# Strassen's seven products for half of the down projection of a two-layer trunk, on one core

## The chip, the cores and the metric

The kernel runs on 1 core of one Trainium2 chip (trn2). The metric is device time in microseconds (us) of one execution; the time of a version is the median over its runs. Besides, one execution is profiled, and its trace gives the start and duration of every instruction. PE is TensorE (PEld its weight loads), DVE is VectorE, ACT is ScalarE, POOL is GpSimd, SP is SyncE, which issues nearly all DMAs.

## The reference

Two layers of a trunk on 256 tokens of width 1024, in float32. Each layer has token mixers (pooling, short convolution, differential attention), a squared-ReLU MLP and an input embedding. The change lies in the MLP:

```python
m = rms_norm(h, norm_mlp_g[i])
h = h + jnp.square(jax.nn.relu(m @ w_up[i])) @ w_down[i]
```

`w_up` is 1024 x 4096 and `w_down` 4096 x 1024 in each of the two layers.

## The kernel before, in words

**Split numbers.** Every operand of a big matmul is a sum of two float32r parts, hi and lo: hi is the rounded value, lo the rest. A product is three matmuls: hi x hi, hi x lo, lo x hi.

**The weight stream.** All big weights come in the order of `weight_plan` (L49), in units of 128 x 1024 numbers; one DMA on SP's queue brings two units (1 MB) into a `stage` tile, of which there are three. `WeightStream.prefetch` (L134) splits a unit: ACT casts it to `whi` (L145), then DVE subtracts to get `wlo` (L146). There are five buffers for each of `whi` and `wlo`; `take` (L153) asks for a unit's successors up to four ahead (`AHEAD = 4`). So the cast of a unit waits until PE has done with the unit whose buffer it takes, and the split of a unit waits for its cast.

**The MLP stage** of a layer (L815 to L875) takes the 4096 hidden features in eight blocks of 512.
- Up units: `first_up` (block 0, four units of 24 matmuls of 256 columns, L285 to L289) and, for blocks 1 to 7, `unit_c` (L292): one unit gives 128 features for all 256 tokens, with 8 matmuls of 512 columns (L298) and 8 of 256 (L300), into one PSUM bank of the pool `bp`, which has four banks. `relu_sq_c` (L828) empties the bank and makes the squared ReLU: an ACT copy (L834), a DVE addition (L835), a DVE multiplication (L836), then `split` (L341: ACT L342, DVE L343).
- Down units: `add_down(j, f)` (L844) multiplies block j, for both token halves, with half f of the 1024 output columns: two units of `unit_a` (L266), each of 12 matmuls of 512 columns (L272 to L274). All blocks add up in four PSUM banks of the pool `acc`, one for each token half t and column half f. `mlp_residual` (L850) scales the sums by 1/mean square and adds them to h (L852).

The order is: the up units of block j, then the down units of block j - 1 for both f. The framework's scheduler sets the final order on each engine; each engine then goes through its list in order.

Of the kernel before, what the change touches and what calls it, by code (L numbers as in the profile page):

```python
# [14 lines left out]
P = 128  # L15
S = 256
# [15 lines left out]
UNIT_COLS = {"A": 512, "B": 256, "C": 128, "P": 512}  # L32
# [16 lines left out]
def weight_plan():  # L49

# [7 lines left out]
    for i in range(DEPTH):  # L58
        def a(name, ks, c):
            plan.extend(("A", name, i, k, c) for k in ks)  # L60
# [27 lines left out]
        for j in range(1, 9):  # L88
            if j < 8:
                plan.extend(("C", "w_up", i, 0, c) for c in range(j * 512, (j + 1) * 512, P))  # L90
            for f in range(2):
                a("w_down", (4 * j - 4, 4 * j - 2), f * 512)
# [5 lines left out]

class WeightStream:

# [5 lines left out]
    def __init__(self, ctx, tc, w):  # L106
        self.nc = tc.nc
        self.w = w
        self.plan = weight_plan()
        self.stage_pool = ctx.enter_context(tc.tile_pool(name="wstage", bufs=self.STAGE_BUFS))  # L110
        self.part_pool = ctx.enter_context(tc.tile_pool(name="wpart", bufs=self.AHEAD + 1))
        self.keep_pool = ctx.enter_context(tc.tile_pool(name="wkeep", bufs=1))
        self.stage = {}
        self.parts = {}
        self.next_dma = 0
        self.next_split = 0
        self.pos = 0

    def load(self, parts=1, between=None):


        if self.next_dma < len(self.plan):
            t = self.stage_pool.tile([P, 2 * UNIT], F32, tag="stage", name="stage")
            src = self.w[self.next_dma // 2]
            n = 2 * UNIT // parts
            for c in range(0, 2 * UNIT, n):
# [3 lines left out]
            for u in range(2):  # L130
                self.stage[self.next_dma + u] = t[:, u * UNIT:(u + 1) * UNIT]
            self.next_dma += 2

    def prefetch(self, upto, between=None):  # L134
        while self.next_split < min(len(self.plan), upto):
# [14 lines left out]
            if u % 2 == 1:  # L150
                self.load()
# [11 lines left out]
def kernel(  # L163
# [42 lines left out]
    def t2(dt=F32):  # L206
        return u2.tile([P, 512], dt, tag="t2", name="t2")

# [57 lines left out]
    def unit_a(accs, xh, xl, name, i, k, c, kx, first, last):  # L266

        wh, wl = ws.take("A", name, i, k, c)
        order = [(t, j) for j in range(2) for t in range(NT)] if first else [(t, j) for t in range(NT) for j in range(2)]
        for t, j in order:  # L270
            tk = slice(t * P, (t + 1) * P)
            nc.tensor.matmul(accs[t], lhsT=xh[:, kx + j, tk], rhs=wh[:, j, :], start=first and j == 0, stop=False)  # L272
            nc.tensor.matmul(accs[t], lhsT=xh[:, kx + j, tk], rhs=wl[:, j, :], start=False, stop=False)  # L273
            nc.tensor.matmul(accs[t], lhsT=xl[:, kx + j, tk], rhs=wh[:, j, :], start=False, stop=last and j == 1)  # L274
# [85 lines left out]
    for i in range(DEPTH):  # L360
# [437 lines left out]
        def mlp_stats():  # L798
            st["r2"] = small(2, "r2")
            nc.vector.reciprocal(out=st["r2"], in_=mean_eps(st["ss"]))  # L800

# [13 lines left out]

        def relu_sq(m):
# [6 lines left out]
            s2 = t2().rearrange("p (m t) -> p m t", t=S)  # L823
# [4 lines left out]
        def relu_sq_c(j, m):  # L828
# [4 lines left out]
            z, s2 = t2()[:, 0:S], t2()[:, 0:S]  # L833
# [9 lines left out]

        def add_down(j, f):  # L844
            for k in (0, 2):
                u = add(lambda k=k: unit_a(get(("d", f)), *st["s", j], "w_down", i, 4 * j + k, f * 512, k,
                                           j == 0 and k == 0, j == 7 and k == 2))
            return u
# [17 lines left out]
        for j in range(1, 9):  # L866
            if j < 8:
# [3 lines left out]
            for f in range(2):  # L871
                u = add_down(j - 1, f)
                if j == 8:
                    at(u, mlp_residual, f)
                    at(u + 1, ple_norm, f)  # L875
                    at(u + 3, lambda f=f: stats_half(st["ss"], f))
# [70 lines left out]
def _pack(inp):  # L947
    import numpy as np

    units = []  # L950
    for kind, name, i, k, c in weight_plan():
        if kind == "P":
            units.append(np.concatenate([inp["pool_w"][i].transpose(1, 0, 2).reshape(P, 4 * P),
                                         inp["p"][i, 0].T.reshape(2, P, S).transpose(1, 0, 2).reshape(P, 2 * S)],
                                        axis=1))
            continue
        wt = inp[name][i]
        nc_ = UNIT_COLS[kind]
        nk = UNIT // nc_
        blk = wt[k * P:(k + nk) * P, c:c + nc_].reshape(nk, P, nc_).transpose(1, 0, 2)  # L960
        units.append(blk.reshape(P, UNIT))
    w = np.stack(units).reshape(-1, 2, P, UNIT).transpose(0, 2, 1, 3).reshape(-1, P, 2 * UNIT)
# [40 lines left out]
```

## Time and profile before

| | us |
|---|---|
| median of 3 runs (lowest to highest) | 859.71 (859.28 to 859.99) |
| the profiled execution, its own time | 859.99 |
| span of its trace (first to last instruction) | 858.2 |
| PE busy in the span | 851.2 (99%) |
| DVE, ACT busy | 582.4 (68%), 454.8 (53%) |
| granted TensorE clock, mean | 1.000 |

A matmul's record is longer than its share of PE, since matmuls overlap: what one costs is the distance from its start to the next one's. The same holds of DVE and ACT, whose instructions start a little before the one ahead of them ends.

### The profile page before, as it was taken

The page shows a single profiled execution, that of the slowest core. Times are in us where ns is not written, and L with a number is a line of the kernel's source. Part 1 is how long each engine was busy: PE and PEld are TensorE (multiplying, and loading weights), DVE is VectorE, ACT ScalarE, POOL GpSimd, SP SyncE. Part 2 cuts the span into 40 slices and gives each one's busy share as a digit, 9 for nine tenths or more (in the row PEclk, how much of TensorE's full clock was granted, in tenths as well). Part 3 has the DMA queues.
Part 4 walks back from the last instruction along what each step waited for, and adds up shares of the span by engine and source line. Part 5 has one row for each costly group of instructions (what it writes and reads, how often), then busy time and mean ns, then how long its engine had stood idle before and what let it go on. Part 6 is the DMA issues. An engine that isn't in the chain of part 4 may idle for free.

```text
span 858.2 us, 11637 instructions
## 1 busy us (share of the span) xinstructions
PE 851.2 (99%) x4564; PEld 733.9 (86%) x4564; DVE 582.4 (68%) x894; ACT 454.8 (53%) x691; POOL 30.6 (4%) x34
## 2 busy tenths in 40 slices
PE   8999999999999999999999999999999999999998
PEld 6989988888888888888889998888889888888887
DVE  5887886656676666666678877955666666666664
ACT  6664564454654444445664746544546544444462
POOL 2400000000000000000023000000000000000000
PEclk9999999999999999999999999999999999999999
DMA  8754536554555555555455444455554555555531
GB/s 319 288 197 157 186 103 216 185 207 174 192 170 185 193 193 196 196 196 189 157 195 196 162 182 147 148 199 192 197 187 157 196 196 197 192 179 186 184 142 50
DMA packets 24103, 158.45 MB, mean 185 GB/s; under 512 B 2800, under 2 KB 3568, under 8 KB 5488
## 3 DMA queue, kind: packets, MB, share of 16 engines
q1 hardware_dynamic: 23904, 157.66, 51.8%
q8 instruction: 36, 0.59, 0.3%
q14 instruction: 19, 0.16, 0.1%
q10 hardware_dynamic: 144, 0.05, 0.0%
HBM read 156.64 MB, written 1.05 MB: 184 GB/s over the span
## 4 chain that ended last, share of the span: by engine, by line
PE 98%; DMA 1%; SPq 0%; DVE 0%; ACT 0%; issue 0%
PE acc L273 20%; PE acc L274 20%; PE acc L272 20%; PE bp L298 12%; PE bp L300 6%; PE bp L289 4%; PE bp L287 4%; PE bp L285 4%; PE tr L321 1%; PE acc L919 1%; DMA stage<-in_w_dram 1%; PE acc L606 1%; PE tr L452 1%; PE tr L698 0%; PE acc L540 0%; PE acc L539 0%
## 5 line engine op out<-in xcount | busy, mean ns | idle before, releaser
L146 DVE TENSOR_TENSOR wlo<-stage,whi 128x1024 fp32r<-128x1024 f32 (+1 forms) x296 | 359.1, 1215 | 239.3 <-ACT whi L145 238.1
L145 ACT CAST whi<-stage 128x1024 fp32r<-128x1024 f32 (+1 forms) x296 | 308.2, 1045 | 348.1 <-PE acc L274 185.3
L272 PE MATMUL acc<-whi,t 128*128 128x512 f32 x752 | 294.1, 393 | 1.4 <-ACT t L311 0.8
L273 PE MATMUL acc<-wlo,t 128*128 128x512 f32 x752 | 293.8, 391 | 0.5 <-DVE wlo L146 0.5
L274 PE MATMUL acc<-whi,t 128*128 128x512 f32 x752 | 290.3, 391 | 0.0
L272 PEld LDWEIGHTS acc<-whi,t 128*128 128x128 f32 x752 | 140.9, 188 | 30.6 <-ACT whi L145 1.8
L273 PEld LDWEIGHTS acc<-wlo,t 128*128 128x128 f32 x752 | 141.3, 188 | 30.0 <-DVE wlo L146 1.8
L274 PEld LDWEIGHTS acc<-whi,t 128*128 128x128 f32 x752 | 140.9, 188 | 29.0
L298 PE MATMUL bp<-t,whi 128*128 128x512 f32 x448 | 122.0, 394 | 0.0
L285 PE MATMUL bp<-t,whi 128*128 128x256 f32 x320 | 90.5, 284 | 0.0
L287 PE MATMUL bp<-t,whi 128*128 128x256 f32 x320 | 90.5, 283 | 0.0
L289 PE MATMUL bp<-t,wlo 128*128 128x256 f32 x320 | 90.5, 283 | 0.0
L298 PEld LDWEIGHTS bp<-t,whi 128*128 128x128 f32 x448 | 77.4, 189 | 11.0
L300 PEld LDWEIGHTS bp<-t,wlo 128*128 128x128 f32 x448 | 68.6, 189 | 9.3
L300 PE MATMUL bp<-t,wlo 128*128 128x256 f32 x448 | 71.2, 281 | 0.0
L287 PEld LDWEIGHTS bp<-t,whi 128*128 128x128 f32 x320 | 61.1, 191 | 0.5
L285 PEld LDWEIGHTS bp<-t,whi 128*128 128x128 f32 x320 | 61.0, 191 | 0.5
L289 PEld LDWEIGHTS bp<-t,wlo 128*128 128x128 f32 x320 | 61.1, 191 | 0.1
L311 ACT ACTIVATE t<-tr,par 128x256 fp32r<-128x256 f32 (+1 forms) x56 | 26.1, 501 | 21.0 <-PE tr L452 8.4
L312 DVE SCALAR_TENSOR_TENSOR t<-tr,par,t 128x256 fp32r<-128x256 f32 (+1 forms) x56 | 27.7, 515 | 5.4 <-ACT t L311 5.1
L343 DVE TENSOR_TENSOR t<-t,t 128x256 fp32r<-128x256 f32 (+1 forms) x64 | 28.6, 449 | 0.0
L342 ACT CAST t<-t 128x256 fp32r<-128x256 f32 (+1 forms) x64 | 27.4, 432 | 0.0
(130 smaller groups left out, 525.1 us busy)
## 6 DMA issues: line engine op xcount, KB each, us to landing
stage<-in_w_dram SPq DMA_DIRECT2D x145, 1024.0 KB, 4.8
stage<-in_w_dram SPq DMA_DIRECT2D x4, 256.0 KB, 5.2
stage<-in_w_dram SPq DMA_DIRECT2D x2, 512.0 KB, 9.3
h<-in_x_dram SPq DMA_DIRECT2D x4, 256.0 KB, 10.6
t<-in_xT_dram SPq DMA_DIRECT2D x1, 512.0 KB, 10.4
out_dram<-h SPq DMA_DIRECT2D x2, 256.0 KB, 2.0
out_dram<-h SPq DMA_DIRECT2D x4, 128.0 KB, 1.8
t<-in_xT_dram SPq DMA_DIRECT2D x1, 384.0 KB, 5.6
```

Source lines behind the costliest of these rows:

```text
L145: self.nc.scalar.copy(out=hi[:, cs], in_=src[:, cs])
L146: self.nc.vector.tensor_sub(out=lo[:, cs], in0=src[:, cs], in1=hi[:, cs].bitcast(F32))
L272: nc.tensor.matmul(accs[t], lhsT=xh[:, kx + j, tk], rhs=wh[:, j, :], start=first and j == 0, stop=False)
L273: nc.tensor.matmul(accs[t], lhsT=xh[:, kx + j, tk], rhs=wl[:, j, :], start=False, stop=False)
L274: nc.tensor.matmul(accs[t], lhsT=xl[:, kx + j, tk], rhs=wh[:, j, :], start=False, stop=last and j == 1)
L285: nc.tensor.matmul(bp[:, m, :], lhsT=wh[:, j, ms], rhs=xh[:, kx + j, :], start=first, stop=False, skip_group_check=True)
L287: nc.tensor.matmul(bp[:, m, :], lhsT=wh[:, j, ms], rhs=xl[:, kx + j, :], start=False, stop=False, skip_group_check=True)
L289: nc.tensor.matmul(bp[:, m, :], lhsT=wl[:, j, ms], rhs=xh[:, kx + j, :], start=False, stop=last, skip_group_check=True)
L298: nc.tensor.matmul(bank, lhsT=wh[:, k, :], rhs=xk[k], start=k == 0, stop=False, skip_group_check=True)
L300: nc.tensor.matmul(bank[:, 1, :], lhsT=wl[:, k, :], rhs=xk[k][:, 0, :], start=False, stop=k == KD - 1, skip_group_check=True)
L312: nc.vector.scalar_tensor_tensor(out=lo, in0=src, scalar=g, in1=hi.bitcast(F32), op0=ALU.mult, op1=ALU.subtract)
L343: nc.vector.tensor_sub(out=lo, in0=src, in1=hi.bitcast(F32))
```

## The change

Blocks are taken in pairs (0,1), (2,3), (4,5), (6,7). For the pairs (0,1) and (4,5) of each layer the down projection is a 2 x 2 matrix product: activations by token half (t) and block, weights by block and column half (f). Instead of eight quarter products of 12 matmuls each it takes Strassen's seven (in Winograd's form), of 12 matmuls each. Product n is two units of a new kind "S", with 6 matmuls a unit.
- **Weight sums.** Products 1, 3 and 2 use a quarter of `w_down` as it is. Products 5, 6, 4 and 7 use sums of quarters, made in two tiles of their own (`fst`, `snd`, 128 x 2048, of the pool t8): quarters (0,0) and (0,1) are loaded into them; after product 1's split DVE adds `snd` to `fst` (product 5); then three DMAs with addition, on POOL's queue, add a further quarter: to `snd` after that addition (product 7), to `fst` after product 5's split (product 6) and again after product 6's (product 4).
- **Activation sums.** `operands` makes four combinations of the squared ReLUs of both blocks, each one DVE instruction of 512 columns and a `split` (one of ACT, one of DVE). The squared ReLUs are kept for it.
- **Where products go.** 2, 3 and 4 add into the `acc` banks of (0,0), (0,1) and (1,0). Products 1, 6 and 7 add up in one `bp` bank ("chain") which DVE reads after each of them; 5 has a `bp` bank ("five") that ACT copies out. From these, `product_out` adds to h what the `acc` banks don't hold.
- **Order.** The eight up units of blocks j and j + 1 come first, then steps of two up units (of blocks j + 2, j + 3) or one half of a down block, with one or two products behind each.
- Units that stay (`add_down` of blocks 2, 3, 6, 7; all up units) have the matmuls that they had.

The core of the diff:

```diff
+GROUPS = (0, 4)
+def mlp_order():
+    order = []
+    for j in range(0, 8, 4):
+        order += [("up", b, m) for b in (j, j + 1) for m in range(4)]
+        ups = [[("up", b, m), ("up", b, m + 1)] for b in (j + 2, j + 3) for m in (0, 2)]
+        downs = [[("down", b, f)] for b in (j + 2, j + 3) for f in range(2)]
+        prods = [[("S", j, n) for n in ns] for ns in ((1,), (5,), (3,), (6,), (7, 2), (4,))]
+        for n, step in enumerate(ups + downs):
+            order += step
+            order += prods[n] if n < len(prods) else []
+    return order
...
     def load(self, parts=1, between=None):
-        if self.next_dma < len(self.plan):
-            t = self.stage_pool.tile([P, 2 * UNIT], F32, tag="stage", name="stage")
...
+            if kind == "S" and prod == 1:
+                if i not in self.sums:
+                    self.sums[i] = self.new_sums()
+                t, second = self.sums[i]
+            elif block:
+                t = self.stage_pool.tile([P, 2 * UNIT], F32, tag="stage", name="stage")
+            else:
+                t = self.sums[i][prod == 7]
...
+            if kind == "S" and prod == 1:
+                self.nc.sync.dma_start(out=second, in_=self.w[self.place[quarter(i, j, 0, 1)]])
...
+    def add_to(self, t, i, j, h, f):
+        self.nc.gpsimd.dma_start(out=t, in_=self.w[self.place[quarter(i, j, h, f)]], accum_op=ALU.add)
+    def sums_after(self, u):
+        kind, prod, i, k, j = self.plan[u]
+        if kind != "S" or k != 2:
+            return
+        fst, snd = self.sums[i]
+        if prod == 1:
+            self.nc.vector.tensor_add(out=fst, in0=fst, in1=snd)
+            self.add_to(snd, i, j, 1, 1)
+        elif prod == 5:
+            self.add_to(fst, i, j, 1, 1)
+        elif prod == 6:
+            self.add_to(fst, i, j, 1, 0)
...
+    ws.new_sums = lambda: [t8().rearrange("p k t -> p (k t)") for _ in range(2)]
...
+    def unit_s(bank, xh, xl, prod, i, k, j, started):
+        wh, wl = ws.take("S", prod, i, k, j)
+        for n in range(2):
+            first = k + n == 0 and not started
+            nc.tensor.matmul(bank, lhsT=xh[:, k + n, :], rhs=wh[:, n, :], start=first, stop=False, ...)
+            nc.tensor.matmul(bank, lhsT=xh[:, k + n, :], rhs=wl[:, n, :], start=False, stop=False, ...)
+            nc.tensor.matmul(bank, lhsT=xl[:, k + n, :], rhs=wh[:, n, :], start=False, stop=k + n == 3, ...)
...
+        def operands(j, step):
+            t0, t1 = slice(0, P), slice(P, S)
+            even, odd = st["f", j], st["f", j + 1]
+            d = t2().rearrange("p (k t) -> p k t", t=P)
+            if step == 0:
+                nc.vector.tensor_sub(out=d, in0=odd[:, :, t1], in1=even[:, :, t1])
...
+            parts = [t2(F32R).rearrange("p (k t) -> p k t", t=P) for _ in range(2)]
+            split(*parts, d)
+            ops[(5, 6, 3, 7)[step]] = parts
...
+        def product_out(n):
+            if n == 5:
+                ops["five"] = t2()
+                nc.scalar.copy(out=ops["five"], in_=tiles.pop(("bp", "five"))...)
+                return
+            chain = tiles[("bp", "chain")].rearrange("p m t -> p (m t)")
+            if n == 1:
+                residual_part(0, 0, chain, "r2")
+                return
+            v = ops["five"] if n == 7 else t2()
+            nc.vector.tensor_add(out=v, in0=chain, in1=ops["five"])
+            if n == 7:
+                residual_part(1, 0, chain, "r2")
...
+            residual_part(n == 7, 1, v, "nr2")
...
-        for j in range(1, 9):
-            if j < 8:
-                for m in range(4):
-                    u = add(lambda j=j, m=m: unit_c(get(("bp", "up", j, m)), st["x"], "w_up", i, j * 512 + P * m))
-                    at(u, relu_sq_c, j, m)
-            for f in range(2):
-                u = add_down(j - 1, f)
...
+        for what, j, n in mlp_order():
+            if what == "up" and j:
+                u = add(lambda j=j, m=n: unit_c(get(("bp", "up", j, m)), st["x"], "w_up", i, j * 512 + P * m))
+                at(u, relu_sq_c, j, n)
+                if j - 1 in GROUPS and n == 3:
+                    for step in range(4):
+                        at(u + 1 + step, operands, j - 1, step)
+            elif what == "down":
+                u = add_down(j, n)
...
+            elif what == "S":
+                add_product(j, n)
```

In the lists below a name's number tells one buffer or bank from another. L244 of the change is the split that was L146; L963, L964 and L459 are L835, L836 and L343 of before; L414 and L416 are L298 and L300.

**DVE, layer 0, up units of blocks 2 and 3.** Before, with two splits and then the empty-and-square work of one up unit in turn:

```order
L146 TENSOR_TENSOR wlo_2510<-stage_2411,whi_2509 128x1024
L146 TENSOR_TENSOR wlo_2540<-stage_2411,whi_2539 128x1024
L835 TENSOR_TENSOR t2_2531<-bp_2508,t2_2531 128x256
L836 SCALAR_TENSOR_TENSOR t2_2532<-t2_2531 128x256
L146 TENSOR_TENSOR wlo_2570<-stage_2458,whi_2569 128x1024
L835 TENSOR_TENSOR t2_2561<-bp_2538,t2_2561 128x256
L343 TENSOR_TENSOR t4_2530<-t2_2532,t4_2529 128x256
L836 SCALAR_TENSOR_TENSOR t2_2562<-t2_2561 128x256
```

And the end of the same place in the change, from the second split of product 5 to the instruction that empties the bank bp_2474 of an up unit:

```order
L244 TENSOR_TENSOR wlo_2528<-t8_2211,whi_2527 128x1024
L1028 SCALAR_TENSOR_TENSOR h00_85<-bp_2510,r2_2309,h00_85 128x512
L244 TENSOR_TENSOR wlo_2547<-stage_2356,whi_2546 128x1024
L459 TENSOR_TENSOR t2_2462<-t2_2459,t2_2461 128x512
L963 TENSOR_TENSOR t2_2467<-bp_2438,t2_2467 128x256
L244 TENSOR_TENSOR wlo_2575<-stage_2356,whi_2574 128x1024
L964 SCALAR_TENSOR_TENSOR t2_2468<-t2_2467 128x256
L996 SCALAR_TENSOR_TENSOR t2_2497<-t2_2459,t4_2275 128x512
L459 TENSOR_TENSOR t4_2466<-t2_2468,t4_2465 128x256
L459 TENSOR_TENSOR t2_2500<-t2_2497,t2_2499 128x512
L244 TENSOR_TENSOR wlo_2605<-stage_2414,whi_2604 128x1024
L963 TENSOR_TENSOR t2_2503<-bp_2474,t2_2503 128x256
```

Splits of shorter units, operand sums (L996, L459 at 512 columns) and an addition to h (L1028) now stand between the instructions that empty the banks.

**PE, the same place in the change**: the last matmul groups of the up unit in bank bp_2573, then product 5 (bank bp_2603).

```order
L414 MATMUL bp_2573<-t8_2154,whi_2475 128x512 x4
L416 MATMUL bp_2573<-t8_2154,wlo_2476 128x256 x4
L385 MATMUL bp_2603<-whi_2511,t2_2461 128x512
L387 MATMUL bp_2603<-wlo_2512,t2_2461 128x512
L389 MATMUL bp_2603<-whi_2511,t2_2462 128x512
```

Product 3 (bank acc_2688) follows 5 at once, before the next up units, and then the first matmul of product 6:

```order
L389 MATMUL acc_2688<-whi_2614,t2_2524 128x512
L385 MATMUL bp_2510<-whi_2690,t2_2499 128x512
L414 MATMUL bp_2628<-t8_2093,whi_2546 128x512 x4
L416 MATMUL bp_2628<-t8_2093,wlo_2547 128x256 x4
L414 MATMUL bp_2628<-t8_2154,whi_2546 128x512 x4
```

With "chain" and "five" held, two of the four `bp` banks are left to the up units there.

## Rows read from the trace of the kernel before

**Rows 1.** The page: busy time of each engine; the chain that ended last
```profile
PE 851.2 (99%) x4564; PEld 733.9 (86%) x4564; DVE 582.4 (68%) x894; ACT 454.8 (53%) x691; POOL 30.6 (4%) x34
...
PE 98%; DMA 1%; SPq 0%; DVE 0%; ACT 0%; issue 0%
PE acc L273 20%; PE acc L274 20%; PE acc L272 20%; PE bp L298 12%; PE bp L300 6%; PE bp L289 4%; PE bp L287 4%; PE bp L285 4%; PE tr L321 1%; PE acc L919 1%; DMA stage<-in_w_dram 1%; PE acc L606 1%; PE tr L452 1%; PE tr L698 0%; PE acc L540 0%; PE acc L539 0%
```

**Rows 2.** Windows, 260.48 to 282.60: busy us (instructions) of PE, PEld, DVE, ACT, POOL, clock, DMA
```profile
260.48:282.60 22.12, 22.12 (x113) 18.82 (x112) 13.90 (x20) 10.70 (x16) 0.00 (x0) 1.00 0.54 191
```

**Rows 3.** All waits of PE in the span: total us, times, longest
```profile
PE tr L224 <- POOL ones L220: 1.0, 1, 1.0
PE acc L272 <- ACT t L311: 0.8, 1, 0.8
PE acc L272 <- ACT whi L145: 0.6, 2, 0.3
PE acc L273 <- DVE wlo L146: 0.5, 1, 0.5
```

**Rows 4.** Waits of DVE and of ACT between 235 and 400
```profile
DVE wlo L146 <- ACT whi L145: 58.1, 58, 1.5
ACT whi L145 <- PE bp L298: 25.3, 20, 1.5
```

**Rows 5.** Timeline of PE: start, us, instruction
```profile
255.72 0.39 PE L272 MATMUL acc<-whi,t 128*128 128x512 f32 x1
...
260.26 0.39 PE L274 MATMUL acc<-whi,t 128*128 128x512 f32 x1
260.48 1.07 PE L298 MATMUL bp<-t,whi 128*128 128x512 f32 x4
...
271.68 0.40 PE L272 MATMUL acc<-whi,t 128*128 128x512 f32 x1
```

**Rows 6.** Timeline of DVE, back to back
```profile
239.94 0.68 DVE L822 TENSOR_SCALAR t<-bp 128x512 f32<-128x512 f32 x1
240.54 0.68 DVE L826 TENSOR_TENSOR t<-t,t 128x512 fp32r<-128x512 f32 x1
241.14 2.35 DVE L146 TENSOR_TENSOR wlo<-stage,whi 128x1024 fp32r<-128x1024 f32 x2
...
248.76 0.42 DVE L343 TENSOR_TENSOR t<-t,t 128x256 fp32r<-128x256 f32 x1
249.09 0.42 DVE L835 TENSOR_TENSOR t<-bp,t 128x256 f32<-128x256 f32 x1
...
398.44 1.40 DVE L852 SCALAR_TENSOR_TENSOR h<-acc,r,h 128x512 f32<-128x512 f32 x2
```

**Rows 7.** Timeline of ACT, back to back
```profile
237.71 1.05 ACT L145 CAST whi<-stage 128x1024 fp32r<-128x1024 f32 x1 [3.96 <-PE bp L287]
238.67 0.63 ACT L824 ACTIVATE t<-t 128x512 fp32r<-128x512 f32 x1
239.20 0.62 ACT L825 ACTIVATE t<-t 128x512 f32<-128x512 f32 x1
...
247.79 0.37 ACT L834 COPY t<-bp 128x256 f32<-128x256 f32 x1
248.06 0.41 ACT L342 CAST t<-t 128x256 fp32r<-128x256 f32 x1
```

**Rows 8.** DMA queue and DMA issues: KB each, median us to landing
```profile
q1 hardware_dynamic: 23904, 157.66, 51.8%
...
stage<-in_w_dram SPq DMA_DIRECT2D x145, 1024.0 KB, 4.8
...
h<-in_x_dram SPq DMA_DIRECT2D x4, 256.0 KB, 10.6
```

**Rows 9.** Groups by line and form: busy us, mean ns of one
```profile
L146 DVE TENSOR_TENSOR wlo<-stage,whi 128x1024 fp32r<-128x1024 f32 x292 | 356.4, 1222 | 237.5 <-ACT whi L145 236.3
...
L835 DVE TENSOR_TENSOR t<-bp,t 128x256 f32<-128x256 f32 x56 | 23.4, 417 | 0.0
```

More of the change, by code (lines that the diff above doesn't have):

```diff
@@ L96, in weight_plan, with quarter, transfer_plan, weight_blocks @@
     return plan
+def quarter(i, j, h, f):
+    return tuple(("A", "w_down", i, 4 * (j + h) + k, 512 * f) for k in (0, 2))
+def transfer_plan():
+    out = []
+    plan = weight_plan()
+    u = 0
+    while u < len(plan):
+        if plan[u][0] != "S":
+            n = 2 if u + 1 < len(plan) and plan[u + 1][0] != "S" else 1
+            out.append((tuple(range(u, u + n)), tuple(plan[u:u + n])))
+        else:
+            n = 2
+            _, prod, i, _, j = plan[u]
+            at = {1: (0, 0), 3: (1, 1), 2: (1, 0)}.get(prod)
+            out.append(((u, u + 1), at and quarter(i, j, *at)))
+        u += n
+    return out
+def weight_blocks():
+    place = {}
+    for _, block in transfer_plan():
+        if block:
+            place.setdefault(block, len(place))
+    for i in range(DEPTH):
+        for j in GROUPS:
+            place.setdefault(quarter(i, j, 0, 1), len(place))
+    return place
 class WeightStream:
@@ L109, in __init__ @@
         self.plan = weight_plan()
+        self.transfers = transfer_plan()
+        self.place = weight_blocks()
+        self.last_unit = {units[-1]: n for n, (units, _) in enumerate(self.transfers)}
         self.stage_pool = ctx.enter_context(tc.tile_pool(name="wstage", bufs=self.STAGE_BUFS))
@@ L119, in load @@
     def load(self, parts=1, between=None):
-        if self.next_dma < len(self.plan):
-            t = self.stage_pool.tile([P, 2 * UNIT], F32, tag="stage", name="stage")
-            src = self.w[self.next_dma // 2]
-            n = 2 * UNIT // parts
-            for c in range(0, 2 * UNIT, n):
+        while self.next_dma < len(self.transfers):
+            units, block = self.transfers[self.next_dma]
+            self.next_dma += 1
+            kind, prod, i, _, j = self.plan[units[0]]
+            size = len(units) * UNIT
+            if kind == "S" and prod == 1:
[4 more added lines that the diff above has]
+                t = self.stage_pool.tile([P, 2 * UNIT], F32, tag="stage", name="stage")
+            else:
+                t = self.sums[i][prod == 7]
+            for n, u in enumerate(units):
+                self.stage[u] = t[:, n * UNIT:(n + 1) * UNIT]
+            if not block:
+                continue
+            src = self.w[self.place[block]]
+            n = size // parts
+            for c in range(0, size, n):
                 self.nc.sync.dma_start(out=t[:, c:c + n], in_=src[:, c:c + n])
@@ new lines, in product @@
+        def product(j, n, k):
+            half = {1: (0, 0), 2: (0, 1), 4: (1, 1)}.get(n)
+            if half:
+                parts = [v[:, :, half[0] * P:(half[0] + 1) * P] for v in st["s", j + half[1]]]
+            else:
+                parts = ops[n]
+            into = {2: (0, 0), 3: (0, 1), 4: (1, 0)}.get(n)
+            if into:
+                t, f = into
+                unit_s(get(("d", f))[t], *parts, n, i, k, j, k > 0 or not begin(t, f))
+            elif n == 5:
+                unit_s(get(("bp", "five"))[:].rearrange("p m t -> p (m t)"), *parts, n, i, k, j, False)
+            else:
+                unit_s(get(("bp", "chain"))[:].rearrange("p m t -> p (m t)"), *parts, n, i, k, j, n > 1)
@@ L848, in add_down, with add_product @@
+        def add_product(j, n):
+            for k in (0, 2):
+                u = add(product, j, n, k)
+            if n in (1, 5, 6, 7):
+                at(u, product_out, n)
             return u
```

109 lines of the change are left out of this document (78 added, 31 removed).

## The prediction, made before the changed kernel ran

> **What bounds the kernel now.** I read the page first, then the waits, then single stretches. The page shows PE busy 99% of the span and on 98% of the chain that ended last; the three lines of the down-type units alone carry 60% of it [rows 1]. The list of PE's waits has four rows, 2.9 us together, and the timeline puts all of them in the program's first 15 us [rows 3]. So in the MLP stage PE never waits, and the time there is the number of matmuls times their distance. One block's round (four up units, four down units) takes 22.12 us, PE full, DVE busy 13.90, ACT 10.70 [rows 2]. DVE and ACT have slack and are paced by PE: DVE's splits wait for ACT's casts (58 times between 235 and 400, 1.0 us each), the casts for PE to give a weight buffer back [rows 4]. A reader should see two things here: that fewer matmuls are worth their full price, and that DVE's slack is 8.2 us in 22.
>
> **Prices.** Each is a distance from start to start.
> - PE: from the first to the last of 21 matmuls of 512 columns 4.54 us, so 0.227 us each; four up units from 260.48 to 271.68, so 2.80 us each [rows 5]. A product is 12 x 0.227 = 2.72 us, one of its units 1.36.
> - DVE: a split of 1024 columns 2.35 - 1.22 = 1.13 us, 512 columns 0.60, 256 columns 0.33, the scaled addition to h 0.66 (1.40 - 0.74) [rows 6] (the 1.22 in [rows 9]). The sum of 2048 columns has no row: twice the split is 2.26, going on by the step from 512 to 1024 (0.53 more per 512) gives 2.19. I take 2.2.
> - ACT: cast of 1024 columns 0.96, 512 columns 0.53, 256 columns 0.27 [rows 7].
>
> **The change part by part.**
> 1. *Matmuls.* Per pair eight quarter products become seven; 12 matmuls go. Four pairs: 48 x 0.227 = **10.9 us saved**, all on the path, since PE is the path. "TensorE: Matmul & The Clock Gate" of the Trainium skill (section "Back-to-back issue gap") gives 131 ns for such a matmul in a sustained stream. By that estimate the saving would be 6.3 us; this trace's 227 ns decides, and the sum uses it.
> 2. *DVE work.* Per pair: six more units to split (14 instead of 8), 6.8 us; the sum of 2048 columns, 2.2; four operands of two instructions of 512 columns, 4.8; for the results three additions to h after chain (1, 6, 7) and a fourth, 4 x 0.66, with two plain additions, 1.2: 3.8. Together 17.6 us. Half a layer (four blocks) had 88.5 us of PE and 55.6 of DVE (four times [rows 2]); it will have 85.8 and 73.2. On average DVE still fits. But it isn't even: a unit of a product gives PE 1.36 us and asks DVE for 1.13, and an up unit asks DVE for 1.13 + 3 x 0.33 = 2.1 of its 2.80. The products, the operands and the sum all lie in the stretch of up units, so this stretch has to be worked out by itself.
> 3. *The stretch up to product 5.* I start where PE has done with the hi buffer of the unit (bank bp_2351) five takes ahead of product 1's first. That is 0.3 us before the unit ends, since its last four short matmuls use lo alone. PE then has six up units and product 1 before product 5: 6 x 2.80 + 2.72 = 19.5 us. On the other side, the cast of product 1's first unit takes 1.05 us; then DVE's list has 30 instructions up to the one that empties bank bp_2474, which product 5 needs: 9 splits (10.2), the 2048-column sum (2.2), 4 of 512 columns (2.4), one addition to h (0.66), 14 of 256 columns and the last (15 x 0.33 = 5.0): 20.5 us. I carried both lists forward, each instruction starting when its engine is free and what it reads or overwrites is ready. DVE waits 1.9 us more on the way. An example: the cast of the second split needs the buffer of the next up unit, 2.8 us after the first one's; DVE has by then 1.13 + 3 x 0.33 + 0.1 = 2.2 us of work, so it waits 0.6. Three waits of 0.4 for ACT and two of 0.1 or less are the rest. Sum: 1.05 + 20.5 + 1.9 + 0.1 for the last one's end, less 0.3 = 23.3 against 19.5. PE waits **3.8 us**: some 1.3 before the second up unit (its bank comes free late too), 2.5 before product 5.
> 4. *The same place in the second half of the layer.* 29 instructions, 9 splits, 14 of 256 columns: 20.2 us and the same kinds of waits: **3.7 us**.
> 5. *Product 6, first half only.* There product 3 and the first matmul of 6 stand directly behind product 5. From the end of 5's second unit PE has 2.72 us. ACT has in that time two casts of units, one operand, one copy and then the cast for product 6: 3 x 0.96 + 0.53 + 0.27 = 3.7, and about 0.3 for the matmul's end and the hand-overs. PE waits 1.3, and 0.3 for a bank behind it: **1.6 us**. In the second half up units stand between 5 and 6 and cover it.
> 6. *Behind that* come down units, 2.72 us of PE with 1.13 of DVE each: DVE catches up, and nothing is left over.
> 7. *Accumulating DMAs.* 12 of 1 MB; no row of before shows one. The tightest is the one between products 5 and 6: from the split's end to the cast of 6 DVE has 7.2 us of its list (and 0.8 of waits) to product 5, PE then 5.4, less the 1.05 of the cast, plus 1.3 of item 5: 13.7 us. Nearest rows: a plain load of 1 MB lands in 4.8 us, twice that (reading the sum as well) is 9.6, and the slowest kind at the crowded start takes 10.6 [rows 8]. All land in time; I take **0**. Queues: SP issues one DMA more; DMA engines go from 52% by 12 in 150, and as much again if an addition costs double, to 56 or 60%. POOL's queue holds nothing else in this stage. Each stage load still has two transfers' time ahead.
> 8. *nr2*, a DVE instruction on two columns, and the order of the down units: beside PE, 0.
>
> Carried forward in the same way, the list of before gives PE no wait in the MLP stage, as in the trace.
>
> **Sum.** Waits 3.8 + 3.7 + 1.6 = 9.1 us per layer, 18.2 in two; less 10.9: 7.3 us more. The profiled execution's own time is 859.99, 0.28 above the median of 859.71, so 867.3 by the one and 867.0 by the other. I forecast **867 us**. Bounds: with none of DVE's waits on ACT (1.9 in each of four places, and item 5 gone) the waits are 7.4 us and the time is 856.2. If DVE's instructions took their full durations (1.22 and 0.42 [rows 9] instead of 1.13 and 0.33), each of the four places costs 2.6 more: 877. The distances were read back to back, as DVE will run here, so I stand near the middle.
>
> **The rivals.**
> - *The average holds* (faster). DVE's waits on ACT close up, because ACT, with half its time free, casts earlier than I carried forward. It decides at 2.7 us of wait per place: below that the saving wins. With none of those waits 856.2, with no wait at all 848.8. For it: DVE's average of 73 in 86. Against: the buffers, not ACT's time, set when a cast may start [rows 4], and DVE's 20.5 us alone exceed PE's 19.5. Chance 0.07.
> - *The accumulated sums come late.* Above 13.7 us from issue to landing every us is paid before product 6 in both layers, and from about 15 in the second halves too: at 16 us some 4 us more, 871; at 20 some 17 more, 884. For it: three such DMAs per pair beside loads that use half the DMA time, and a queue that before doesn't use at all. Against: item 7. A rule speaks for it: "SBUF — State Buffer" of the Trainium skill (section "SBUF: two separate sides") says that DMAs issued by GpSimd have their descriptors written through a port that DVE can lock, so that they start late beside a busy DVE. It exempts additions and subtractions of two tensors in the section on interference, and these fill DVE's list here; no run so far shows either. Chance 0.15.
> - *Hand-overs cost more than I carried*, up to the 877 above, from semaphores or slower DVE instructions beside more DMA traffic. Chance 0.08.
>
> **How the numbers follow.** The forecast has the rest, 0.70, and by itself lies between 862 and 872 (a tenth of an us on each of ten hand-overs per place, four places). The range must reach to part of the rivals: down to **860**, which leaves out most of the first, up to **880**, which leaves out the later half of the second. A measurement here can tell 0.2%, 1.7 us, from no change. Faster by more than that needs the waits below 9.2 us, half of mine: 0.06; within: 0.04; slower: 0.90.
>
> **What would show it.** Right: PE's waits, before 2.9 us in all, reach some 20; their rows name the up units' first matmul line (L414) and the products' (L385) with DVE's bank-emptying line L963 and ACT's cast L243 as releasers; they lie in four places, around 265, 357, 693 and 784 us, of 3.7 to 5.4 us each; PE's busy share falls by 2 points; DVE is near full for some 24 us ahead of each. The accumulating DMAs land in 6 to 12 us. Wrong: waits of the casts L243 on an accumulating DMA (the second rival), no PE waits there (the first), or a granted clock under 1.00 behind the waits; before it was 1.00 in every slice.

## The result and the profile after

The changed kernel takes 872.49 us (median of 4 runs, 871.66 to 873.98) against 859.85 us for the kernel before beside it (4 runs, 859.28 to 860.19): a ratio of 1.015, 95% interval 1.0138 to 1.0163. It is slower, as forecast, and inside the range of 860 to 880, but 5.5 us above the forecast of 867.0 and just outside the 862 to 872 that the forecast by itself allowed; the range reached further up only for the rivals' sake. The profiled execution took 872.22 us, its span 870.5.

The page of the changed kernel, busy time and chain, against [rows 1]:

```profile
PE 846.5 (97%) x4516; PEld 727.9 (84%) x4516; DVE 651.5 (75%) x980; ACT 491.9 (57%) x735; POOL 41.2 (5%) x46
...
PE 92%; DVE 4%; ACT 2%; issue 1%; DMA 1%; SPq 0%; ACTq 0%
```

PE has 48 matmuls fewer, as said. But the span is 12.3 us longer, and DVE and ACT now stand on the chain. All waits of PE in the span of the changed kernel (total us, times, longest), against [rows 3]:

```profile
PE bp L385 <- DVE t L963: 9.6, 4, 2.4
PE bp L414 <- DVE t L963: 5.4, 6, 1.3
PE bp L385 <- ACT whi L243: 2.3, 2, 1.1
PE tr L325 <- POOL ones L321: 1.0, 1, 1.0
...
```

From the fourth row on it is the start of the program as before, 2.5 us in all. The first three are new: 17.3 us in twelve waits. The timeline of PE in the changed kernel shows the first place (first layer, first half), wait by wait, in the brackets:

```profile
261.97 1.15 PE L414 MATMUL bp<-t,whi 128*128 128x512 f32 x4 [1.33 <-DVE t L963]
...
267.39 0.47 PE L385 MATMUL bp<-whi,t 128*128 128x512 f32 x1 [2.39 <-DVE t L963]
...
274.22 0.50 PE L385 MATMUL bp<-whi,t 128*128 128x512 f32 x1 [1.15 <-ACT whi L243]
274.96 0.47 PE L414 MATMUL bp<-t,whi 128*128 128x512 f32 x1 [0.24 <-DVE t L963]
```

These are an up unit whose bank comes late, product 5, product 6 and the up unit behind it. The second layer repeats them to 0.04 us, and the second halves have the first two (1.12 and 2.39).

In the second layer something follows that the first doesn't have. The same timeline at 695 us:

```profile
695.08 0.47 PE L385 MATMUL bp<-whi,t 128*128 128x512 f32 x1 [2.39 <-DVE t L963]
...
696.12 0.63 PE L387 MATMUL bp<-wlo,t 128*128 128x512 f32 x1
696.54 0.63 PE L389 MATMUL bp<-whi,t 128*128 128x512 f32 x1
...
699.73 0.40 PE L387 MATMUL acc<-wlo,t 128*128 128x512 f32 x1
699.97 0.40 PE L389 MATMUL acc<-whi,t 128*128 128x512 f32 x1
```

From 696.12 to 696.54 is 0.42 us, from 699.73 to 699.97 is 0.24, as everywhere else. Windows of the changed kernel (columns as in [rows 2]; the clock is the figure behind POOL) show the reason, before and behind the 2.39 us waits:

```profile
265.00:270.00 5.00, 2.61 (x12) 2.21 (x13) 4.20 (x8) 2.87 (x5) 0.00 (x0) 1.00 0.95 301
...
691.00:696.00 5.00, 2.61 (x15) 2.14 (x14) 4.22 (x9) 2.75 (x5) 0.00 (x0) 1.00 0.99 247
696.00:699.40 3.40, 3.40 (x10) 2.65 (x9) 2.69 (x4) 1.66 (x2) 0.00 (x0) 0.50 0.43 181
...
788.20:791.60 3.40, 3.27 (x8) 2.63 (x9) 2.65 (x5) 1.31 (x3) 0.00 (x0) 0.50 0.62 255
```

The granted clock fell to half, from 2.4 to 1.2 GHz, at two of the four waits of 2.39 us, for 3.4 us each time: 1 us behind the third wait, and from the last 0.1 us of the fourth on. PE is busy there but starts a matmul every 0.42 us instead of 0.23, so I estimate a fall at some 1.7 us, 3.4 for the two. Before, the clock was 1.00 in every slice.

The transfers of the changed kernel (queues, and issues with KB and median us to landing), against [rows 8], and the 2048-column sum (minimum, median and maximum duration in ns):

```profile
q0 software_dynamic: 1728, 12.58, 7.6%
...
stage<-in_w_dram SPq DMA_DIRECT2D x136, 1024.0 KB, 4.8
t<-in_w_dram POOLq DMA_DIRECT2D x12, 1024.0 KB, 8.8
```
```profile
L225 DVE TENSOR_TENSOR t<-t,t x4: 2281/2284/2285, 249.5 to 770.3; 128x2048 f32<-128x2048 f32 x4
```

The accumulating DMAs land in 8.8 us, and neither PE nor DVE nor ACT has a row of waits for them. So on the trace alone the waits came as predicted, and the open question was what the other 5 us are. My theory for the runs: DVE's list sets the waits, and a wait of over 2 us can cost the clock as well. The rivals: the clock is an accident of the run (A), the accumulated sums or their traffic (B).

### The profile page after: what moved, and what is told of

It is laid out like the page before. It is cut to its first block, busy times and chain, and to the rows that moved or that the text cites. A ratio compares the mean times of both kernels' runs of the same rounds, so it can differ in the third digit from the quotient of the medians.

```text
span 870.5 us, 11751 instructions
## 1 busy us (share of the span) xinstructions
PE 846.5 (97%) x4516; PEld 727.9 (84%) x4516; DVE 651.5 (75%) x980; ACT 491.9 (57%) x735; POOL 41.2 (5%) x46
## 4 chain that ended last, share of the span: by engine, by line
PE 92%; DVE 4%; ACT 2%; issue 1%; DMA 1%; SPq 0%; ACTq 0%
PE acc L376 49%; PE bp L414 11%; PE bp L416 5%; PE bp L403 4%; PE bp L405 4%; PE bp L401 4%; DVE wlo L244 2%; PE bp L385 2%; PE bp L387 1%; PE bp L389 1%; PE tr L437 1%; ACT whi L243 1%; PE acc L1128 1%; PE acc L387 1%; PE acc L389 1%
## 5 line engine op out<-in xcount | busy, mean ns | idle before, releaser
L244 DVE TENSOR_TENSOR wlo<-stage,whi 128x1024 fp32r<-128x1024 f32 (+1 forms) x280 | 339.1, 1214 | 168.4 <-ACT whi L243 166.6
L243 ACT CAST whi<-stage 128x1024 fp32r<-128x1024 f32 (+1 forms) x280 | 291.5, 1045 | 273.2 <-PE acc L376 147.7
L376 PE MATMUL acc<-whi,t 128*128 128x512 f32 x1248 | 396.7, 393 | 0.9 <-ACT whi L243 0.6
L376 PEld LDWEIGHTS acc<-whi,t 128*128 128x128 f32 x1248 | 233.7, 188 | 49.4 <-ACT whi L243 1.6
L376 PE MATMUL acc<-wlo,t 128*128 128x512 f32 x624 | 243.6, 390 | 0.5 <-DVE wlo L244 0.5
L376 PEld LDWEIGHTS acc<-wlo,t 128*128 128x128 f32 x624 | 117.2, 188 | 24.9 <-DVE wlo L244 1.6
L414 PE MATMUL bp<-t,whi 128*128 128x512 f32 x448 | 122.4, 395 | 5.4 <-DVE t L963 5.4
L414 PEld LDWEIGHTS bp<-t,whi 128*128 128x128 f32 x448 | 77.3, 189 | 17.7 <-issue 6.6
L416 PEld LDWEIGHTS bp<-t,wlo 128*128 128x128 f32 x448 | 68.5, 189 | 9.3
L416 PE MATMUL bp<-t,wlo 128*128 128x256 f32 x448 | 71.2, 281 | 0.0
L244 DVE TENSOR_TENSOR wlo<-t,whi 128x1024 fp32r<-128x1024 f32 x40 | 48.9, 1222 | 11.0 <-ACT whi L243 11.0
L243 ACT CAST whi<-t 128x1024 fp32r<-128x1024 f32 x40 | 42.1, 1051 | 25.8 <-PE bp L414 15.9
L459 DVE TENSOR_TENSOR t<-t,t 128x256 fp32r<-128x256 f32 (+1 forms) x80 | 39.6, 497 | 3.1 <-ACT t L458 2.8
L385 PE MATMUL bp<-whi,t 128*128 128x512 f32 x64 | 26.9, 420 | 11.8 <-DVE t L963 9.6
```

What stands on the lines that cost most here:

```text
L243: self.nc.scalar.copy(out=hi[:, cs], in_=src[:, cs])
L244: self.nc.vector.tensor_sub(out=lo[:, cs], in0=src[:, cs], in1=hi[:, cs].bitcast(F32))
L376: nc.tensor.matmul(accs[t], lhsT=lhs[:, kx + j, tk], rhs=rhs[:, j, :], start=begins[t] and j == 0 and n == 0, stop=last and j == 1 and n == 2,
L385: nc.tensor.matmul(bank, lhsT=xh[:, k + n, :], rhs=wh[:, n, :], start=first, stop=False, skip_group_check=True)
L414: nc.tensor.matmul(bank, lhsT=wh[:, k, :], rhs=xk[k], start=k == 0, stop=False, skip_group_check=True)
L416: nc.tensor.matmul(bank[:, 1, :], lhsT=wl[:, k, :], rhs=xk[k][:, 0, :], start=False, stop=k == KD - 1, skip_group_check=True)
```

## Experiments

Eight kernels ran. The kernel before, beside them, took 859.88 us (e1 to e4) and 859.94 (e5 to e8), 13 runs each. All times are medians.

**e1: without the 2048-column sum.**

```diff
         if prod == 1:
-            self.nc.vector.tensor_add(out=fst, in0=fst, in1=snd)
             self.add_to(snd, i, j, 1, 1)
```

> The VectorE sum of 2048 columns per pair is left out, so product 5 multiplies quarter (0,0) alone; all else, transfers and matmuls too, is as in the changed kernel. My theory (VectorE's list in the stretch up to product 5 sets the waits, and each wait of 2.4 us costs more through the granted clock): the list ahead of each of the four places is 2.2 us shorter, the waits near 267, 359, 695 and 788 us before product 5 shrink from 2.4 us to under 1 us each; PE's waits fall by some 8 us in all, and with no wait of 2 us left the granted clock stays at 1.00 in every stretch, which gives back a further 3.4 us: 872.5 - 7.9 - 3.4 = 861 us. Rival A (the waits alone, the half clock is a chance of the run): 864.6 us, with clock rows at 0.66 to 0.84 still there. Rival B (the accumulated sums come late): the waits before product 5 have nothing to do with the VectorE sum, time stays above 870.

Measured: 861.42 us (10 runs), ratio 1.002, interval 1.001 to 1.003. The list of PE's waits in this kernel, and the span with its mean clock:

```profile
PE bp L384 <- ACT whi L242: 4.7, 4, 1.2
PE acc L388 <- DVE t L458: 2.5, 4, 0.6
...
PE acc L384 <- ACT t L457: 1.4, 4, 0.3
```
```profile
core 0: 859.9 us, clock 1.000
```

The waits of 2.39 us are gone, 8.6 us of short ones are left, and the clock stays at 1.00. One instruction of 2.28 us per pair, 9.1 us of DVE in all, was worth 11.1 us of time: more than its own duration. Rival A (864.6) misses by 3.2 us, and the mean clock is 0.999 or 1.000 in all ten executions, where the changed kernel's four have 0.994 to 0.996. With the accumulating DMAs still there B is out.

**e4: without the accumulating DMAs.**

```diff
     def add_to(self, t, i, j, h, f):
-        self.nc.gpsimd.dma_start(out=t, in_=self.w[self.place[quarter(i, j, h, f)]], accum_op=ALU.add)
+        pass
```

> The twelve accumulating DMAs are left out, so the weights of products 6 and 7 are incomplete sums; all other work and every transfer by SyncE stays. My theory: nothing waits for them and they slow nothing: 872.5 us within 1, the same waits row by row. Rival B (sums come late, or their traffic slows VectorE or the loads): the waits before product 6 (1.15 us each in the first halves) and part of the 2.4 us waits go, 866 us or less.

Measured: 872.26 us, ratio 1.0147 (1.0131 to 1.0162). PE's waits in this kernel:

```profile
PE bp L385 <- DVE t L963: 9.6, 4, 2.4
PE bp L414 <- DVE t L963: 5.4, 6, 1.3
PE bp L385 <- ACT whi L243: 2.3, 2, 1.1
```

These three rows are the same as with them. The accumulating DMAs cost nothing here.

**e3: two more VectorE instructions of 2048 columns per pair.**

```diff
             self.nc.vector.tensor_add(out=fst, in0=fst, in1=snd)
+            self.nc.vector.tensor_sub(out=fst, in0=fst, in1=snd)
+            self.nc.vector.tensor_add(out=fst, in0=fst, in1=snd)
```

> Two more VectorE instructions of 2048 columns per pair (the second tile is subtracted again and added again, so the value stays): 4.4 us more VectorE per place, four places. My theory: two of the four places pay all but what slack there is; carried forward, 12.5 us more of waits, 17.6 at most, with waits of up to 6.6 us before product 5 in all four places, and a clock at half behind each of them (four times some 1.7 us instead of two): 872.5 + 12.5 + 3.4 = 888 us. Rival A (clock unrelated): 885. Rival (the average holds, VectorE's slack takes it up): under 876.

Measured: 884.20 us, ratio 1.0284 (1.0269 to 1.0299). In this kernel's list of PE's waits one row is left in the MLP stage; the timeline shows the first of its four waits, with the matmul that follows the up unit, and windows show the clock at the first and the third:

```profile
PE bp L416 <- DVE t L965: 24.9, 4, 6.4
```
```profile
267.33 2.04 PE L416 MATMUL bp<-t,whi 128*128 128x512 f32 x4 [6.40 <-DVE t L965]
...
272.25 0.40 PE L387 MATMUL bp<-whi,t 128*128 128x512 f32 x1
```
```profile
265.00:271.80 6.80, 4.47 (x13) 3.73 (x14) 6.04 (x13) 2.32 (x5) 0.42 (x1) 0.50 1.03 224
698.50:708.70 10.20, 6.01 (x18) 5.17 (x19) 9.09 (x15) 5.12 (x11) 0.86 (x1) 0.50 0.97 219
```

Half clock begins within each of the four waits and lasts 6.8 us, in the third place 10.2. The up unit behind the wait takes 272.25 - 267.33 = 4.92 us instead of 2.80. The direction is right, the size is not: I expected 12.5 us more of waits, and there are 24.9 - 17.3 = 7.6. At half clock PE gives DVE 2.1 us to catch up within that one unit, and the wait before product 6 is gone; I had carried the lists forward at full clock. That this is why the waits are smaller is read from the timelines; no run tests it. The time comes 4 us under the forecast by another road: smaller waits, longer half clock.

**e2: ten matmuls of zeros, one up unit ahead of product 5.** `FILL` is 10, `zero` a tile of zeros; the lines that make them are left out here.

```diff
             elif n == 5:
+                if k == 0:
+                    for _ in range(FILL):
+                        nc.tensor.matmul(tiles[("bp", "chain")].rearrange("p m t -> p (m t)"), lhsT=zero,
+                                         rhs=st["s", j][0][:, 0:2, :], start=False, stop=False,
+                                         skip_group_check=True)
```

> Ten matmuls of 512 columns with weights of zero are added per pair (2.3 us of TensorE each time, into the running sum of products 1, 6 and 7), one up unit ahead of product 5; the result is the same. My theory: the waits before product 5 become shorter by part of what TensorE spends on the fillers; carrying the lists forward the waits fall from 17 to some 13 us and the fillers cost 9.1 us, so with the clock as it was the time would rise by 3.4 us to 876; but with a TensorE that is busier in the stretch the granted clock should stay at 1.00, which gives 3.4 us back: about 872, no slower than the changed kernel within 1.5 us. Rival A (the clock's fall has nothing to do with the waits): 876 us with clock rows under 1.00 still there. Rival C (TensorE is simply the bound, and its waits don't matter): +9.1 us, 881.6.

Measured: 872.65 us (871.41 to 876.01), ratio 1.0156 (1.0133 to 1.0179). That is the time that my theory gave, but not by its road: the waits fell to 11.0 us instead of 13, and the clock did fall, once in the profiled execution and, by its mean clock, twice in another. That the two errors cancel is luck. The fillers did not land as meant either: in the second halves they took the place of both waits (and a wait of 1.13 us before product 6 appeared), but in the first halves they replaced the 1.33 us wait and left the 2.39 us one behind them. The timeline of this kernel:

```profile
260.00 2.49 PE L1028 MATMUL bp<-t,zero 128*128 128x512 f32 x10
...
267.69 0.47 PE L388 MATMUL bp<-whi,t 128*128 128x512 f32 x1 [2.39 <-DVE t L966]
```

What this run does tell comes from its four executions, one program with different clocks. Mean clock 1.000 goes with spans of 869.6 and 870.2 us, 0.998 with 871.5, 0.996 with 874.2. One stretch of 3.4 us at half is 0.002 of the mean clock, so the same program has none, one or two of them. What one costs is read within the profiled execution below; the spans scatter too much for it (the kernel before differs by 1.9 us among 13 executions without a fall).

**e5: the matmuls of zeros in the wait itself**, in the first halves only. They need product 6's first operand, which is ready when the wait begins.

```diff
+                if k == 0 and j == 0:
+                    for _ in range(FILL):
+                        nc.tensor.matmul(tiles[("bp", "chain")].rearrange("p m t -> p (m t)"), lhsT=zero,
+                                         rhs=ops[6][0].rearrange("p k t -> p (k t)"), start=False, stop=False,
+                                         skip_group_check=True)
```

> In the first half of each layer ten matmuls of 512 columns with weights of zero stand in the wait before product 5 itself (they need product 6's first operand, which is ready when the wait begins); they add zeros to the running sum. The second halves are as in the changed kernel. Product 5 can start no earlier than before, so by the lists the time is unchanged. My theory (the granted clock falls behind a wait of 2.4 us, here in layer 1): the fall at 696 us goes, because TensorE works through that wait; the one at 788 us stays; 872.5 - 1.7 = 870.8 us, half clock for 3.4 us in one place instead of two. Rival A (the clock has nothing to do with that wait): both stretches of half clock stay, 872.5. Rival (the fillers delay product 5): 873 to 874.

Measured: 870.09 us (870.05 to 871.34), ratio 1.0124 (1.0108 to 1.0141). The kernel with 20 more matmuls is faster than the changed kernel by 2.4 us: its slowest execution is under the other's fastest, 871.66, though the intervals of the ratios touch. Of the 2.2 us between the profiled executions 1.4 lie in the MLP stages (one fall fewer, by the table in the next section); most of the rest lies ahead of them, where no filler stands. Windows of this kernel: the unfilled wait of the first layer and what is behind it, then the filled one of the second layer, then the stretch behind the unfilled one there:

```profile
355.00:359.40 4.40, 2.00 (x11) 1.60 (x10) 3.61 (x7) 2.34 (x5) 0.00 (x0) 1.00 0.97 268
359.40:362.80 3.40, 3.40 (x9) 2.65 (x8) 2.93 (x5) 2.40 (x5) 0.00 (x0) 0.50 0.33 137
690.00:695.00 5.00, 4.53 (x24) 3.89 (x25) 4.21 (x7) 2.35 (x4) 0.00 (x0) 1.00 1.05 231
695.00:700.00 5.00, 4.93 (x22) 3.77 (x21) 4.57 (x8) 3.08 (x5) 0.00 (x0) 1.00 0.67 246
...
789.00:794.00 5.00, 5.00 (x23) 4.13 (x23) 4.76 (x7) 4.27 (x8) 0.00 (x0) 1.00 0.40 128
```

Behind the filled wait the clock stays. One half of my forecast failed: the fall at 788 us did not stay, one came at 359 us in its place. The same wait has no fall in the changed kernel, so which of the waits of 2.4 us bring one can't be read from the list of instructions. Two filled waits without a fall prove little by themselves, since 6 of 13 unfilled ones had none either; what they do show is that the fillers cost nothing.

**e6: only the order.** Four up units of the next block come ahead of product 1, a down unit pair stands between products 1 and 5, and up units between 5, 3 and 6. U, D and X list up units, down units and products.

```diff
-        ups = [[("up", b, m), ("up", b, m + 1)] for b in (j + 2, j + 3) for m in (0, 2)]
-        downs = [[("down", b, f)] for b in (j + 2, j + 3) for f in range(2)]
-        prods = [[("S", j, n) for n in ns] for ns in ((1,), (5,), (3,), (6,), (7, 2), (4,))]
-        for n, step in enumerate(ups + downs):
-            order += step
-            order += prods[n] if n < len(prods) else []
...
+        order += U(j, 0, 1, 2, 3) + U(j + 1, 0, 1, 2, 3) + U(j + 2, 0, 1, 2, 3) + X(1)
+        order += D(j + 2, 0) + X(5) + U(j + 3, 0, 1) + X(3) + U(j + 3, 2, 3) + X(6) + D(j + 2, 1) + X(7, 2) + X(4) + D(j + 3, 0) + D(j + 3, 1)
```

> Only the order of up units, down units and products is changed: products 1 and 5 come after the first four up units of the next block, with one down unit pair between them and up units spread between the later products. The same matmuls, VectorE instructions and DMAs. My theory: VectorE's work per stretch is less crowded ahead of products; carried forward, PE's waits fall from 17 to 9 us, the longest from 2.4 to 1.3, so the clock stays at 1.00: 872.5 - 7.9 - 3.4 = 861 us. Rival (the amount of VectorE work decides, not its place): no change, 872. Rival A (clock unrelated): 864.6.

Measured: 860.44 us (10 runs), ratio 1.001 (1.0001 to 1.0019). The new waits of PE in this kernel:

```profile
PE acc L385 <- DVE wlo L242: 4.1, 4, 1.0
PE bp L383 <- DVE t L961: 3.2, 4, 0.8
```

Two more, of 0.24 and 0.78 us, lie between the two layers; e8 below shows the same two. With the same matmuls, VectorE instructions and transfers, the order alone is worth 12 us. The rival (amount, not place) is out.

**e7: the sums by DMA alone**, in the order of the change. The two tiles are loaded plainly and added to ahead of product 1; one plain load and one accumulating DMA per pair come on top.

```diff
             if kind == "S" and prod == 1:
-                self.nc.sync.dma_start(out=second, in_=self.w[self.place[quarter(i, j, 0, 1)]])
+                self.nc.sync.dma_start(out=fst, in_=src)
+                self.nc.sync.dma_start(out=snd, in_=self.w[self.place[quarter(i, j, 0, 1)]])
+                self.add_to(fst, i, j, 0, 1)
+                self.add_to(snd, i, j, 1, 1)
...
-        if prod == 1:
-            self.nc.vector.tensor_add(out=fst, in0=fst, in1=snd)
-            self.add_to(snd, i, j, 1, 1)
-        elif prod == 5:
+        if prod == 5:
```

> The order of the changed kernel, but the two sums of product 5's and 6's weights are made ahead by accumulating DMAs on the two tiles (loaded plainly, then added to), product 1's weights are loaded to a stage tile as any other, and VectorE's sum of 2048 columns is gone. Two more accumulating DMAs... one more plain load of 1 MB and one more accumulating DMA per pair. My theory: as with the sum left out, 861 to 863 us (waits of some 10 us, none of 2 us, clock at 1.00), since transfers have time to spare. Rival B (accumulated sums come late): over 866, with waits of casts on an accumulating DMA.

Measured: 865.65 us (864.51 to 867.05), ratio 1.0069 (1.0054 to 1.0084): over my 863. Three of the four places are as in e1, but for one wait of 0.99 us instead of 0.61. In the first one ACT's timeline has a cast that waits for a load, PE's timeline a wait of 2.60 us before product 5, and the windows full DMA engines up to it (0.98, at 0.63 in the changed kernel) and half clock behind the wait:

```profile
252.00 1.05 ACT L243 CAST whi<-stage 128x1024 fp32r<-128x1024 f32 x1 [3.94 <-DMA stage<-in_w_dram]
```
```profile
265.87 0.76 PE L385 MATMUL bp<-whi,t 128*128 128x512 f32 x1 [2.60 <-DVE t L963]
```
```profile
226.00:252.00 26.00, 26.00 (x183) 24.24 (x182) 17.34 (x29) 14.72 (x27) 1.93 (x2) 1.00 0.98 310
...
265.20:272.00 6.80, 6.13 (x15) 4.64 (x16) 4.99 (x9) 2.56 (x4) 0.00 (x0) 0.50 0.81 246
```

It was not the accumulated sum that came late, as B has it, but a plain stage load beside the extra transfers. That is read from the trace of one execution; no run moved those loads. By the mean clocks, 0.995 to 1.000, not every execution has the half clock; the one at 1.000 still took 864.51.

**e8: the order of e6 and the sums of e7 together.**

> The order of e6 and the sums by DMA of e7 together. My theory: VectorE's list then keeps up everywhere, carried forward PE has no wait of more than 0.3 us in the MLP stage, so the full price of the 48 matmuls is saved: 859.9 - 10.9 = 849 us, up to 851. Rival (matmuls saved are not worth 0.227 us each, or a new bound appears): 855 to 860. Rival B (late sums with four accumulating DMAs per pair): over 855, with casts waiting on an accumulating DMA.

Measured: 851.37 us (850.62 to 852.65), ratio 0.9903 (0.9889 to 0.9918), faster than both kernels and 0.4 above my 851. Busy time, the only wait of PE in the MLP stage, and the landing of the accumulating DMAs in this kernel:

```profile
PE 841.4 (99%) x4516; PEld 725.1 (85%) x4516; DVE 639.8 (75%) x976; ACT 489.8 (58%) x735; POOL 44.6 (5%) x50
...
t<-in_w_dram POOLq DMA_DIRECT2D x16, 1024.0 KB, 9.2
```
```profile
PE bp L412 <- DVE t L961: 0.3, 1, 0.3
```

PE has two more waits that the kernels before and changed don't have, between the two layers (timeline):

```profile
425.94 0.41 PE L435 MATMUL tr<-csb,h 128*128 128x128 f32 x2 [0.24 <-DVE h L1098]
427.13 0.50 PE L374 MATMUL acc<-whi,t 128*128 128x512 f32 x1 [0.78 <-ACT t L425]
```

They come with the order of e6, which has them too. The late load of e7 is in this trace as well:

```profile
251.19 1.05 ACT L241 CAST whi<-stage 128x1024 fp32r<-128x1024 f32 x1 [3.94 <-DMA stage<-in_w_dram]
```

Here only the wait of 0.3 us follows it, at 268.5 us; the other three places have none. I read this from the order, in which product 5 comes later; it was not tested. DVE's share of the span is 75%, the same as in the changed kernel.

## Why the prediction was right or wrong

I take the time of the MLP stages from the timelines of PE: from the first matmul of block 1's up units, start to start over 832 matmuls (808 with the change, 828 in e2, 818 in e5), to one of the last down matmuls of the layer.

| us | layer 0 | layer 1 |
|---|---|---|
| before | 162.57 | 162.56 |
| changed kernel | 167.13 | 170.22 (two falls of the clock) |
| e2 | 168.77 | 170.40 (one fall) |
| e5 | 168.78 (one fall) | 167.18 |
| e8 | 157.94 | 157.12 |

The ends of the second layer's stretch, in the kernel before and in e8:

```profile
658.14 0.63 PE L298 MATMUL bp<-t,whi 128*128 128x512 f32 x2
...
820.70 0.39 PE L273 MATMUL acc<-wlo,t 128*128 128x512 f32 x1
```
```profile
653.79 0.40 PE L412 MATMUL bp<-t,whi 128*128 128x512 f32 x1
...
810.91 0.39 PE L374 MATMUL acc<-wlo,t 128*128 128x512 f32 x1
```

By the prediction's own steps:

1. *Matmuls, 10.9 us saved.* Right. In e8's second layer, where PE never waits, the stretch is 5.44 us shorter for 24 matmuls: 0.227 us each, the row's price. e8's span, 848.8, is only 9.4 us under 858.2 for other reasons: 0.8 us are lost around the wait of 0.3 us in the first layer, and 1.5 us between the layers, at the two waits there (262.07 us from stretch to stretch instead of 260.59). The program's start and end give 0.8 of it back. The profiled execution is also the fastest of e8's four; by the medians the gain is 8.6. The estimate from "TensorE: Matmul & The Clock Gate" of the Trainium skill, 6.3 us, is further off than the row's price.
2. *DVE's work.* The sum of 2048 columns was put at 2.2; it takes 2.28 and the next instruction starts 2.20 later.
3. *Up to product 5, 3.8 us:* 1.33 + 2.39 = 3.72 in the list of waits. DVE is busy 21.98 of the 24 us ahead of product 5, and waits for ACT 2.0 us there, against the 1.9 that were carried forward.
4. *Second half, 3.7:* 1.12 + 2.39 = 3.51. One addition of 0.33 us fewer than in step 3 gives 3.5 by the prediction's own prices; its 3.7 was slightly high.
5. *Product 6, 1.6, first half only:* 1.15 + 0.24 = 1.39, and no such wait in the second halves.
6. *Nothing behind:* right.
7. *Accumulating DMAs, 0:* right by e4. They land in 8.8 us, inside the bounds and under the slack of 13.7. The rule of "SBUF — State Buffer" of the Trainium skill (section "SBUF: two separate sides") about DMAs of GpSimd beside a busy DVE is not seen at work here, where two-tensor operations fill DVE's list; that agrees with its exemption.

So the waits came to 17.3 us in the list, of the 18.2 in the sum. But a wait costs more than the list says. The first layer of the changed kernel, which has no fall, takes 167.13 - 157.12 = 10.0 us longer than e8's second layer, at six waits listed with 8.62 us: 0.23 us more for each. The list counts a wait from the end of the matmul's record ahead of it, which is longer than its share (0.28 us against 0.12 for 256 columns), and the matmul behind a wait is followed after 0.30 us instead of 0.23. Twice 10.0 is 20.0 us, 1.8 more than the sum had.

The step that failed is the **sum** itself: it priced a wait at PE's idle time alone and left out the clock. The prediction names a granted clock under 1.00 only among the signs that would make it wrong. The second layer of the changed kernel has the same waits as the first to 0.06 us in all, and takes 3.1 us longer: the two falls. The one fall in e2 shows as 170.40 - 168.77 = 1.6 us, the one in e5 as 168.78 - 167.13 = 1.6 us. In spans: 858.2 - 10.9 + 20.0 + 3.1 = 870.4, against 870.5 measured. My sum was 858.2 + 7.3 = 865.5; of the 5.0 that it is short, 3.1 are the clock and 1.8 the waits.

Is the clock's fall an effect of the waits? e1 and e6 have the same TensorE work without a wait over 1.2 us, and no fall. By the mean clocks this holds in all ten executions of each (0.999 or 1.000); the changed kernel's four have 0.994 to 0.996, e3's four 0.981 to 0.983. In e5 the filled waits have none. In the profiled executions 7 of 13 waits of 2.39 to 2.60 us brought one (2 of 4 in the changed kernel and in e4, 1 of 2 in e2 and e5, 1 of 1 in e7), 4 of 4 of 6.06 to 6.40 us, and no wait of up to 1.34 us. I take it as shown that waits of this length can bring the fall. What picks the waits was not tested: by the mean clocks, e2's four executions had none, one and two falls. "TensorE: Matmul & The Clock Gate" of the Trainium skill (section "Part 1: The HAM clock gate") says that the gate watches activity in a count that runs freely, so that the point of a transition varies from run to run; e2's executions agree with that.

The rivals: *the average holds* fell, since DVE is only 75% busy and PE waits 17.3 us; e6 and e8 show when the average does hold, namely when the order spreads the work. *Late sums* fell by e4. *Hand-overs cost more*: true for the 1.8 us.

## What to carry to other kernels

A price of work moved to an engine with slack belongs to the stretch where it falls: carry that engine's list forward, instruction by instruction, to the point where the bound engine needs its last result, and move the order before moving the work. A single wait of 2.4 us or more on TensorE is to be priced with a possible half clock behind it (here 1.6 us for each fall at 2.4 us); between 1.34 and 2.39 us no wait was measured. Several short waits are cheaper: the three in each place of e1, 2.1 us together, brought no fall. Each restart costs too, here some 0.2 us above the listed wait. A saving that looks lost may only be out of place: 48 matmuls were worth a loss of 12.6 us in one order and a gain of 8.6 in another, with one VectorE sum given to the DMA engines.

## What was not expected of the hardware

Ten matmuls of zeros in a wait of 2.4 us cost nothing (e5: 167.18 us for the second layer's stretch, against 167.13 for the changed kernel's first, which has no fall either). Half clock lasted 3.4 us at waits of 2.4 us, 6.8 at one of 2.60 (e7), and 6.8 to 10.2 at waits of over 6 us (e3), though PE was busy for most of it. An accumulating DMA of 1 MB into SBUF, three or four per pair beside loads, landed in 8.3 us (e1, e3) to 9.7 us (e7) by the kernels' medians, against 4.8 for a plain load: about twice, as the prediction's bound had put it.
